# Two GpSimd steps wait for VectorE, and four engines get other orders, in a one-core attention kernel

## The chip, the core and the metric

The kernel runs on one core of a Trainium2 chip. The core has a TensorE (matrix products, PE in the profile, with PEld for its weight loads), a VectorE (DVE), a ScalarE (ACT), a GpSimd (POOL) and a SyncE (SP), which only issues transfers here. Each engine takes its own list of instructions strictly in order and waits for the others by semaphores. The metric is the time of one execution in device microseconds, as the median of several runs. A profiled execution has a span, from its first to its last instruction, and a time of its own, which is a little longer.

## The reference

```python
Q, K, V: (8 batches, 12 heads, 512 rows, 64 columns), float32;  tau = 0.1
Q_norm = Q / (norm(Q, axis=-1) + 1e-10);  K_norm = K / (norm(K, axis=-1) + 1e-10)
scores = Q_norm @ K_norm^T / tau
weights = softmax(scores, axis=-1)
out = weights @ V
```

That is 96 heads of attention with cosine scores. The scores are bounded by 1/tau, so the kernel takes no maximum out of the exponential.

## The kernel before

The 96 heads are worked as 48 pairs, s = 0 to 47. The text names a step by its kind, the pair, and what follows:

- LD.s.w loads Q (w = 0) or K (w = 1) of a pair, LV.s loads V (SyncE, L320 and L323). VC.s copies V to bfloat16 (GpSimd, L582).
- SQ.s squares Q and K (GpSimd, L346, 1024 columns). SSQ.s.w adds up those squares on TensorE for most K halves (8 matmuls, L363); RED.s.w ends the sum on VectorE (L370 after an SSQ, L374 straight from the squares).
- NEW.g.k are the steps of an inverse square root for a group of up to four pairs (VectorE, L399 to L408). Groups from the twelfth on have four pairs: 28 to 31 are group 14, 32 to 35 are 15, 36 to 39 are 16.
- SCL.s.w scales Q or K by the inverse norm to bfloat16 (L432): Q on VectorE, K on GpSimd, except in the pairs that K_ON_DVE lists.
- TR.s.w transposes them on TensorE (four matmuls, L438), EVA.s copies the transposed pair out of PSUM (VectorE, L446).
- SCO.s.c makes the scores of one quarter c of the keys for both heads (two matmuls, L561), EXP.s.c takes their exponential (ScalarE, L577, 1024 columns). There are two score buffers: the scores of one quarter need the exponential of the quarter two earlier to be done.
- PV.s.h.t multiplies by V for one head h and one quarter t of the queries (four matmuls, L594); a 65th column of ones gives the sum of the weights. RCP.s.h inverts the sum (L613), NRM.s.h multiplies by it (VectorE, L615). ST.s stores the pair (SyncE). Each head parity has one PSUM bank for its products, so PV.s.h.0 waits for the NRM of the products that stood there before, and for a RED whose SSQ used a corner of the bank.

In two places ScalarE's work is moved elsewhere. The last quarter of the keys of pairs 30 and 43 has no EXP: SCX makes its scores, X.s.h.k prepares them on VectorE (L496, L499), and a polynomial takes the place of the exponential. For pair 30 (form "B") Y.30.0 to Y.30.2 run on GpSimd (L517, L518), Y.30.3 and Y.30.4 on VectorE (L519). Both of these take two float32 operands of 128 x 1024 from SBUF. Pair 43 (form "A") has Y.43.0 to Y.43.3 on GpSimd, Y.43.4 (L519) and Y.43.5 (L518) on VectorE. PV_LATER puts the products of pair 30 behind those of pair 31.

Nothing is scheduled at run time. A table ORDER gives each engine's list as numbers of the steps in the sequence in which `P.add` made them, and `Program.run` (L52) writes the lists with the waits that each step's `needs` ask for. The order in which TensorE takes its work is such that two to four PV, TR or SSQ steps stand between one SCO and the next; a step among them that has to wait holds up the SCO behind it. The tail is the last pair: its last quarter is exponentiated in three pieces (512, 128 and 384 columns, L572), each with its own products (L630), RCP (L641), NRM (L649, one on ScalarE at L645) and store (L653).

"The head" is what each list holds up to about the seventh pair.

Of the kernel before, what the change touches and what calls it, by code (L numbers as in the profile page):

```python
# [5 lines left out]
ALU = mybir.AluOpType  # L6
# [102 lines left out]
def bass_cosine_similarity_attention_kernel(  # L109
# [10 lines left out]
    NT = SEQ // 128  # L120
# [57 lines left out]
    def key(name, s, *rest):  # L178
        return (name, s) + rest if s >= 0 else None
# [30 lines left out]
    for (s, c), (turns, _) in OFF.items():  # L210
        for h in range(2):
            turn_user.setdefault(turns[h], []).append((s, h))
# [93 lines left out]
    def pair(s):  # L306
# [119 lines left out]
        for w in range(2):  # L426
# [4 lines left out]
                  [("NEW", g, (7 if direct_r(g) else 6) if acts and dve else 6 + w + (dve and w))] + ([("UNIT", s)] if s in off_of and w == 0 else []) + ([("TR", 0, w, 0), ("TR", 0, w, 1)] if s == R_QN else [key("TR", s - R_QN, w)]),  # L431
# [4 lines left out]
            def tr(e, w=w):  # L436
                for t in range(NT):
# [4 lines left out]
            P.add(("TR", s, w), "pe", "tr", T0 - PERIOD + 0.9 * TR_AT[w],  # L442
                  [("SCL", s, w), ("EVA", s - 1) if s > 1 else ("EVA", 0, 0, 1), "eye"]
                  + [x_last(*u) for u in turn_user.get(s - 1, [])[-1:]], tr)
        P.add(("EVA", s), "dve", "eva", T0 - 1.5, [("TR", s, 0), ("TR", s, 1)] + scos(s - R_QT),
              lambda e: e.tensor_copy(  # L446
                  out=qt[iqt][:, :, :, :].rearrange("p w t x -> p (w t x)"),
                  in_=t_ps[:, :, :, :].rearrange("p w t x -> p (w t x)")))
# [30 lines left out]
    def poly(s, c, at):  # L479
# [6 lines left out]
        for h in range(2):  # L486
            users = turn_user[turns[h]]
# [10 lines left out]
            P.add(("X", s, h, 1), "dve", "x1", at + h, [("X", s, h, 0)],
                  lambda e, h=h, z1=z1: e.scalar_tensor_tensor(out=z1, in0=xp[:, h, :], scalar=a0 - LIFT * UNIT, in1=x_ps, op0=ALU.add, op1=ALU.subtract))  # L499
            if form != "D":  # L500
                continue
            two, half = xp[:, h, :].bitcast(bf16), xw[:, h, :]
            chain = [
                lambda e: e.tensor_tensor(out=x_ps, in0=x_ps, in1=x_ps, op=ALU.mult),
                lambda e, two=two, half=half: e.scalar_tensor_tensor(out=half, in0=x_ps, scalar=a3, in1=two, op0=ALU.add, op1=ALU.mult),
                lambda e: e.scalar_tensor_tensor(out=x_ps, in0=x_ps, scalar=2.0 * a1, in1=x_ps, op0=ALU.add, op1=ALU.mult),
                lambda e, h=h, half=half: e.scalar_tensor_tensor(
                    out=et[s % R_ET][:, c, h, :], in0=x_ps, scalar=a1 * a1 + a2, in1=half, op0=ALU.add, op1=ALU.mult)]
            for k, step in enumerate(chain):
                P.add(("X", s, h, k + 2), "dve", "x1", at + h + 0.6 * k,  # L510
                      [("X", s, h, k + 1)] + (done(1) if k == 1 else []) + ([key("PV", s - R_ET, i, NT - 1) for i in range(2)] if k == 3 else []), step)
        if form == "D":
            return
# [107 lines left out]
    def last(s, T0):  # L621
        iq, iet, io = s % R_QK, s % R_ET, s % R_O
        spare = t_ps[:, :, :, :].rearrange("p w t x -> p (w t x)").bitcast(f32)
        for k, (h, lo, hi) in enumerate(PIECES):
            bank = spare if k == 2 else o_ps[h]
            for c in range(NT):
                def pv(e, h=h, lo=lo, hi=hi, c=c, bank=bank):
                    for t in range(lo, hi):
# [8 lines left out]
                           + (([("EVA", s)] if k == 2 else bank_free[s, h]) if c == 0 else [("PV", s, k, c - 1)]), pv)  # L637
# [40 lines left out]
PV_LATER = {30:1}  # L678
EARLY = 4
# [19 lines left out]

def late(s):  # L700
    return LATE * max(0.0, 1 - s / LATE_TO)


def slack(s, most):
# [14 lines left out]
    ),  # L719
    "pool": (  # L720
# [113 lines left out]
```

## Time and profile before

| what | value |
|---|---|
| median of 3 runs | 189.42 us (189.26, 189.42, 190.38) |
| the profiled execution's own time | 190.04 us |
| its span | 188.1 us |
| granted TensorE clock, mean over the span | 0.999 |
| HBM read, written | 37.75 MB, 12.58 MB |
| DVE chain, ACT chain (shares of the chain that ended last) | 63%, 26% |

The page gives each engine's busy time with its share of the span. A group of instructions has its source line, engine, operation, written and read tile, shape, count, then busy time and mean duration, then the idle time of its engine just before it. The timeline gives start and length in us; neighbours of one kind are merged into one row with their count, and a bracket tells the idle time before a row and what ended it. The table of stages gives start and end, length, and the busy time of each engine with its count of instructions. Instructions of one engine overlap at their ends, so a duration is longer than the distance to the next start.

### The profile page before, as it was taken

To read this page: it belongs to the slowest core of one execution; us is meant where nothing else is said; L and a number is where in the kernel's file an instruction comes from. 1 tells how busy PE (TensorE), PEld (TensorE's weight loads), DVE (VectorE), ACT (ScalarE), POOL (GpSimd) and SP (SyncE) were. 2 spreads that over 40 slices of the span, in tenths; PEclk is the share of its full clock that TensorE was granted. 3 is DMA by queue.
4 is the path that set the end of the run, shared out by engine and by line. 5 is a ranking of instruction groups with operands and counts; after the bars stand their busy time and mean duration, and the time that the engine had idled before them with its cause. 6 is when DMAs were issued, how large, how long until landed. Compare 5 with 4: busy or idle time off the path is not lost.

```text
span 188.1 us, 6663 instructions
## 1 busy us (share of the span) xinstructions
PE 176.0 (94%) x2705; PEld 108.9 (58%) x2705; DVE 175.4 (93%) x567; ACT 181.5 (96%) x213; POOL 163.4 (87%) x148
## 2 busy tenths in 40 slices
PE   6898899999998999999999999899999999999993
PEld 2454566666555666656666655466565566556562
DVE  2689999999999999999999999999999999999853
ACT  5799999999999999999999999999999999999993
POOL 5399999999999999999999999999999999298000
PEclk9999999999999999999999999999999999999999
DMA  5999999999999999998999999579971031133334
GB/s 149 345 349 349 349 348 372 377 353 352 353 375 380 379 351 327 345 334 268 315 352 347 360 375 369 183 223 300 357 247 56 6 110 59 57 114 112 116 123 159
DMA packets 52446, 50.76 MB, mean 270 GB/s; under 512 B 3264, under 2 KB 52416, under 8 KB 52416
## 3 DMA queue, kind: packets, MB, share of 16 engines
q1 hardware_dynamic: 51984, 50.05, 81.0%
q8 instruction: 21, 0.34, 0.8%
q10 hardware_dynamic: 432, 0.30, 0.5%
q14 instruction: 9, 0.07, 0.1%
HBM read 37.75 MB, written 12.58 MB: 268 GB/s over the span
## 4 chain that ended last, share of the span: by engine, by line
DVE 63%; ACT 26%; PE 3%; DMA 3%; issue 3%; SPq 1%
ACT et L577 25%; DVE qn L432 14%; DVE ob L615 11%; DVE qt L446 11%; DVE nps L374 10%; DVE rd L613 3%; DMA qk<-in_K_dram 3%; DVE nps L370 3%; DVE nps L399 2%; DVE nps L400 2%; PE ops L594 2%; DVE nps L404 1%; PE scps L561 1%; DVE ys L404 1%; DVE ys L408 1%
## 5 line engine op out<-in xcount | busy, mean ns | idle before, releaser
L577 ACT ACTIVATE et<-scps 128x1024 bf16<-128x1024 f32 x185 | 170.4, 1190 | 0.2
L346 POOL TENSOR_TENSOR sq<-qk 128x1024 bf16<-128x1024 f32 x44 | 85.0, 1943 | 0.1
L561 PE MATMUL scps<-qt 64*128 64x512 bf16 x372 | 72.5, 386 | 4.3 <-ACT et L577 2.5
L594 PE MATMUL ops<-vb,et 128*128 128x65 bf16 x1504 | 73.4, 195 | 1.0 <-DVE ob L615 0.5
L594 PEld LDWEIGHTS ops<-vb,et 128*128 128x128 bf16 x1504 | 55.2, 98 | 31.9 <-issue 18.4
L432 DVE TENSOR_TENSOR qn<-qk,nps 128x512 bf16<-128x512 f32 x61 | 39.9, 676 | 0.6 <-ACT nps L391 0.6
L615 DVE TENSOR_TENSOR ob<-ops,rd 128x256 f32<-128x256 f32 x94 | 38.6, 416 | 0.4
L432 POOL TENSOR_TENSOR qn<-qk,rk 128x512 bf16<-128x512 f32 x33 | 34.2, 1045 | 4.3 <-DVE rk L404 4.1
L438 PE MATMUL tps<-ident,qn 128*128 128x128 bf16 x376 | 33.3, 220 | 0.9 <-DVE qn L432 0.6
L446 DVE COPY qt<-tps 128x1024 bf16<-128x1024 bf16 x47 | 32.0, 681 | 0.2 <-PE tps L438 0.2
L374 DVE TENSOR_REDUCE nps<-sq 128x8 f32<-128x512 bf16 x46 | 30.6, 679 | 0.0
L561 PEld LDWEIGHTS scps<-qt 64*128 64x128 bf16 x372 | 18.2, 92 | 20.6 <-ACT et L577 6.5
L582 POOL TENSOR_SCALAR vb<-vf 128x512 bf16<-128x512 f32 x48 | 29.4, 632 | 0.1
L438 PEld LDWEIGHTS tps<-ident,qn 128*128 128x128 bf16 x376 | 21.6, 98 | 11.7 <-issue 4.9
L363 PE MATMUL ops<-sq,ident 128*128 128x64 bf16 x384 | 19.2, 193 | 1.1 <-POOL sq L340 0.6
L613 DVE RECIPROCAL rd<-ops 128x4 f32<-128x4 f32 x94 | 15.8, 173 | 2.6 <-PE ops L594 2.6
L363 PEld LDWEIGHTS ops<-sq,ident 128*128 128x128 bf16 x384 | 14.2, 98 | 5.5 <-issue 2.0
L370 DVE TENSOR_REDUCE nps<-ops 128x8 f32<-128x64 f32 x46 | 9.8, 216 | 0.0
L400 DVE SCALAR_TENSOR_TENSOR nps<-nps,ys 128x32 f32<-128x32 f32 (+2 forms) x34 | 7.0, 206 | 0.4
L340 POOL TENSOR_TENSOR sq<-qk 128x512 bf16<-128x512 f32 (+1 forms) x5 | 4.7, 954 | 3.0 <-DMA qk<-in_K_dram 2.7
L399 DVE TENSOR_TENSOR nps<-nps,ys 128x32 f32<-128x32 f32 (+2 forms) x34 | 7.0, 206 | 0.3
L192 PE MATMUL ops<-warm_in,ident 128*128 128x512 bf16 x8 | 3.6, 628 | 1.4 <-POOL eps L185 1.4
(67 smaller groups left out, 71.2 us busy)
## 6 DMA issues: line engine op xcount, KB each, us to landing
vf<-in_V_dram SPq DMA_DIRECT2D x48, 256.0 KB, 6.8
qk<-in_Q_dram SPq DMA_DIRECT2D x47, 256.0 KB, 5.5
qk<-in_K_dram SPq DMA_DIRECT2D x47, 256.0 KB, 6.6
out_dram<-ob SPq DMA_DIRECT2D x47, 256.0 KB, 4.2
qk<-in_Q_dram SPq DMA_DIRECT2D x2, 128.0 KB, 2.5
qk<-in_K_dram ACTq DMA_DIRECT2D x2, 128.0 KB, 2.8
out_dram<-ob SPq DMA_DIRECT2D x1, 128.0 KB, 1.7
out_dram<-ob SPq DMA_DIRECT2D x1, 96.0 KB, 1.6
```

Source lines behind the costliest of these rows:

```text
L346: lambda e: e.tensor_tensor(out=sqf, in0=data, in1=data, op=ALU.mult))
L363: last = e.matmul(out=o_ps[bank][:, 320:384], lhsT=ident[:, :], rhs=sq[iqs][:, 8 * w : 8 * w + 8, 8 * k : 8 * k + 8], start=(k == 0), stop ...
L374: lambda e, w=w, dst=dst: e.tensor_reduce(out=dst, in_=sq[iqs][:, 8 * w : 8 * w + 8, :], axis=AX.X, op=ALU.add))
L432: lambda e, w=w, r=r: e.tensor_tensor(out=qn[iqn][:, w].rearrange("p t h d -> p h t d"), in0=qk[iq][:, w].rearrange("p h (t d) -> p h t d" ...
L438: last = e.transpose(t_ps[:, w, t, :], qn[iqn][:, w, t].rearrange("p h d -> p (h d)"), ident[:, :])
L446: lambda e: e.tensor_copy(out=qt[iqt][:, :, :, :].rearrange("p w t x -> p (w t x)"), in_=t_ps[:, :, :, :].rearrange("p w t x -> p (w t x)")))
L561: last = e.matmul(out=sc_ps[:, 2 * b + h, :], lhsT=qt[iqt][64 * h : 64 * h + 64, 1, c, :], rhs=qt[iqt][64 * h : 64 * h + 64, 0, :, :], sta ...
L577: lambda e, c=c, b=b: e.activation(out=et[iet][:, c, :, :], in_=sc_ps[:, 2 * b : 2 * b + 2, :], func=ACT.Exp, scale=math.log(2.0) / UNIT i ...
L582: lambda e: e.tensor_scalar(out=vb[:, iq, :, :, 0:DIM].rearrange("p c h d -> p h c d"), in0=vf[iv][:, :, :].rearrange("p h (c d) -> p h c ...
L594: last = e.matmul(out=o_ps[h][:, 65 * t : 65 * t + 65], lhsT=et[iet][:, c, h, 128 * t : 128 * t + 128], rhs=vb[:, iq, c, h, :], start=(c = ...
L613: (lambda e, h=h, grid=grid: e.reciprocal(out=rd[io][:, h, :], in_=grid[:, :, DIM])))
L615: lambda e, h=k, grid=grid: e.tensor_tensor(out=ob[io][:, h], in0=grid[:, :, 0:DIM], in1=rd[io][:, h, :].unsqueeze(2).to_broadcast([128, N ...
```

## The change

Most lines of the diff change nothing in the built program: a removed polynomial form "D" that no pair used, a way of transposing by DMA for pairs in TURNED, which is empty, loads issued by ScalarE for pairs in BY_SCALAR, which is empty, and the helper `by_pe`, which returns its argument while TURNED is empty. What is left are two added waits and other orders. The set of instructions, their shapes and their engines are the same.

```diff
+    for waits, held in HOLD.items():
+        P.ops[waits].needs.append(held)
     P.run()
...
+HOLD = {("SQ",36,0):("Y",30,3),("VC",44):("Y",30,4)}
...
+TURNED = range(0)
+BY_SCALAR = ()
...
 ORDER = {
     "sp": (
...
-        "428 429 353 471 470 396 430 69 472 504 153 505 547 548 108 581 582 506 624 625 549 658 659 583 700 701 "
+        "428 429 353 471 470 396 430 69 472 504 505 547 548 581 582 506 624 625 549 658 659 583 700 701 626 734 "
...
     "act": (
...
-        "1725 1727 1755 1757 1759 1761 1789 1791 1793 1795 1822 1824 1826 1830 1828 1829 1851 1852 "
+        "1725 1727 1755 1757 1759 1761 1789 1791 1793 1795 1822 1824 1826 1828 1830 1829 1851 1852 "
```

So SQ.36.0 on GpSimd now waits for Y.30.3 on VectorE, and VC.44 on GpSimd for Y.30.4. The other differences are positions in the lists. Counted by place, 116 of SyncE's 193 places hold another step, 89 of GpSimd's 144, 326 of VectorE's 567 and 460 of TensorE's 734; the first of them stand at SyncE's 39th place (LD.12.1 for ST.2), GpSimd's 28th (SCL.7.1 for VC.7), VectorE's 86th (RED.8.0 for SCL.7.0) and TensorE's 91st (TR.7.1 for TR.7.0). ScalarE's list changes in two places at its end: the 512-column piece of the last quarter now comes before the 128-column piece.

The places that matter below, in names:

```
GpSimd around pair 30
before  SCL.29.1 VC.37 VC.36 SCL.31.1 VC.38 SQ.33 SQ.34 SQ.35 Y.30.0 Y.30.1 VC.39 Y.30.2
        SCL.32.1 SQ.36 SCL.34.1 SQ.37 VC.40 SQ.38 SQ.39 SCL.35.1
after   SQ.32 SQ.35 SCL.28.1 VC.35 SCL.29.1 VC.37 VC.34 SCL.31.1 SQ.33 SQ.34 SQ.37 Y.30.0 VC.36 Y.30.1
        Y.30.2 SCL.32.1 SQ.36 SCL.34.1 SCL.35.1 VC.44 VC.43 SQ.39 SQ.38 VC.42 VC.40 VC.45 VC.41
VectorE ahead of NRM.9.0
before  RED.14.0 SCL.12.0 RED.14.1 RCP.8.1 NRM.9.0
after   SCL.12.0 NEW.8.8 RED.14.1 RCP.9.0 SCL.12.1 NRM.9.0 SCL.13.0 EVA.12 RED.14.0
VectorE around Y.30
before  SCL.32.0 NEW.15.8 Y.30.3 RCP.27.1 SCL.33.1 NRM.27.1 EVA.32 SCL.33.0 RCP.28.1 NRM.28.1 RCP.29.0
        SCL.34.0 NRM.29.0 RED.36.1 EVA.33 RCP.29.1 Y.30.4 RCP.31.0 RED.37.1 NRM.29.1 NRM.31.0 EVA.34
after   NEW.15.8 SCL.32.0 Y.30.3 EVA.32 SCL.33.1 RCP.27.1 SCL.33.0 NRM.27.1 SCL.34.0 EVA.33 RCP.29.0 RED.36.1
        NRM.29.0 RCP.28.1 Y.30.4 NRM.28.1 EVA.34 RED.37.0 RCP.31.0 RED.37.1 NRM.31.0 RCP.29.1
TensorE ahead of some scores
before  PV.23.1.2 TR.28.1 TR.28.0 SCO.26.3          after   TR.28.0 TR.28.1 SCO.26.3
before  PV.30.0.0 PV.31.1.0 PV.31.1.1 PV.30.0.1 SCO.33.2 ... PV.31.1.3 SSQ.38.1 PV.32.0.0 SCO.34.0
after   PV.29.1.2 PV.29.1.3 TR.35.1 SCO.33.2 PV.30.0.0 PV.30.0.1 PV.30.0.2 PV.30.0.3 SCO.33.3
        ... PV.32.0.2 PV.32.0.3 SSQ.38.1 SSQ.39.1 SCO.34.2
SyncE ahead of LV.44
before  ST.24 LV.42 ST.21 ST.26 LD.45.0 ST.23 LD.45.1 ST.25 LV.43 LD.46.0 ST.22 LD.46.1 LD.47.0 LV.44
after   LV.42 LD.45.0 LD.45.1 LV.43 LD.46.0 ST.22 ST.23 LD.46.1 ST.21 LD.47.0 LV.44 ST.25 ST.27 ST.26
VectorE's end
before  NRM.46.1 RCP.47.2 RCP.47.0 NRM.47.0 RCP.47.1 NRM.47.1
after   NRM.46.1 RCP.47.0 RCP.47.2 NRM.47.0 RCP.47.1 NRM.47.1
```

More of the change, by code (lines that the diff above doesn't have):

```diff
@@ L211, in bass_cosine_similarity_attention_kernel @@
         for h in range(2):
-            turn_user.setdefault(turns[h], []).append((s, h))
+            turn_user.setdefault(by_pe(turns[h]), []).append((s, h))
+    for users in turn_user.values():
+        users.sort()
     session, attached, early = {}, {}, []
@@ L318, in pair @@
                 continue
-            P.add(("LD", s, w), "sp", "ld1" if s == 1 else "ld", s, [*([("CST", 0, i) if w else ("SCL", 0, 0, i) for i in range(2)] + [("SQ", 0, w, 0), ("SQ", 0, w, 1)] if s == R_QK else [key("SCL", s - R_QK, w), *(squares(s - R_QK, w) if s >= R_QK else [])])],
+            P.add(("LD", s, w), "act" if (s, w) in BY_SCALAR else "sp", "ld1" if s == 1 else "ld", s, [*([("CST", 0, i) if w else ("SCL", 0, 0, i) for i in range(2)] + [("SQ", 0, w, 0), ("SQ", 0, w, 1)] if s == R_QK else [key("SCL", s - R_QK, w), *(squares(s - R_QK, w) if s >= R_QK else [])])],
                   lambda e, w=w, x=x: e.dma_start(out=qk[iq][:, w], in_=src(x, s)),
@@ L430, in pair @@
             P.add(("SCL", s, w), "dve" if dve else "pool", "sclq" if dve else "sclk", T0 - (2.85 if w and not dve else 2.55) - slack(s, M_SCL),
-                  [("NEW", g, (7 if direct_r(g) else 6) if acts and dve else 6 + w + (dve and w))] + ([("UNIT", s)] if s in off_of and w == 0 else []) + ([("TR", 0, w, 0), ("TR", 0, w, 1)] if s == R_QN else [key("TR", s - R_QN, w)]),
+                  [("NEW", g, (7 if direct_r(g) else 6) if acts and dve else 6 + w + (dve and w))] + ([("UNIT", s)] if s in off_of and w == 0 else []) + ([("TR", 0, w, 0), ("TR", 0, w, 1)] if s == R_QN else [key("TR", s - R_QN, w)] if s - R_QN not in TURNED else [("EVA", s - R_QN)]),
                   lambda e, w=w, r=r: e.tensor_tensor(
@@ L440, in tr @@
                 return last
[L442 to L448, printed above, removed]
+            if s not in TURNED:
+                P.add(("TR", s, w), "pe", "tr", T0 - PERIOD + 0.9 * TR_AT[w],
+                      [("SCL", s, w), ("EVA", by_pe(s - 1)) if s > 1 else ("EVA", 0, 0, 1), "eye"]
+                      + [x_last(*u) for u in turn_user.get(by_pe(s - 1), [])[-1:]], tr)
+        if s in TURNED:
+            P.add(("EVA", s), "sp", "trd", s + TURN_AT, [("SCL", s, 0), ("SCL", s, 1)] + scos(s - R_QT),
+                  lambda e: e.dma_start_transpose(
+                      out=qt[iqt][:, :, :, :].rearrange("p w t x -> p (w t) x"),
+                      in_=qn[iqn][:, :, :, :, :].rearrange("p w t h d -> p (w t h d)")), slot=f"qt{iqt}")
+        else:
+            P.add(("EVA", s), "dve", "eva", T0 - 1.5, [("TR", s, 0), ("TR", s, 1)] + scos(s - R_QT),
+                  lambda e: e.tensor_copy(
+                      out=qt[iqt][:, :, :, :].rearrange("p w t x -> p (w t x)"),
+                      in_=t_ps[:, :, :, :].rearrange("p w t x -> p (w t x)")))
         rest(s)
@@ L486, in poly @@
         for h in range(2):
-            users = turn_user[turns[h]]
+            users = turn_user[by_pe(turns[h])]
             before = [x_last(*users[users.index((s, h)) - 1])] if users.index((s, h)) else []
@@ L492, in sco @@
                                 rhs=qt[s % R_QT][64 * h : 64 * h + 64, 0, :, :], start=True, stop=True)
-            P.add(("SCX", s, h), "pe", "sco1", at + h, [("EVA", s), ("EVA", turns[h])] + before, sco)
+            P.add(("SCX", s, h), "pe", "sco1", at + h, [("EVA", s), ("EVA", by_pe(turns[h]))] + before, sco)
             P.add(("X", s, h, 0), "dve", "x1", at + h, [("SCX", s, h)] + done(2),
                   lambda e, h=h: e.tensor_scalar(out=xp[:, h, :], in0=x_ps, scalar1=BIG, scalar2=LIFT * UNIT - BIG, op0=ALU.add, op1=ALU.add))
-            z1 = x_ps if form == "D" else xz[:, h, :]
             P.add(("X", s, h, 1), "dve", "x1", at + h, [("X", s, h, 0)],
[L499 to L513, printed above, removed]
+                  lambda e, h=h: e.scalar_tensor_tensor(out=xz[:, h, :], in0=xp[:, h, :], scalar=a0 - LIFT * UNIT, in1=x_ps, op0=ALU.add, op1=ALU.subtract))
         flat = lambda t: t[:, :, :].rearrange("p h q -> p (h q)")
@@ L636, in last @@
                            ([("EXP", s, c, k)] if c == NT - 1 else exps(s, c)) + [("VC", s)]
-                           + (([("EVA", s)] if k == 2 else bank_free[s, h]) if c == 0 else [("PV", s, k, c - 1)]), pv)
+                           + (([("EVA", by_pe(s))] + [x_last(*u) for u in turn_user.get(by_pe(s), [])[-1:]] if k == 2 else bank_free[s, h]) if c == 0 else [("PV", s, k, c - 1)]), pv)
                 op.count = hi - lo
@@ L678 @@
 PV_LATER = {30:1}
+TURNED = range(0)
+TURN_AT = 6.5
 EARLY = 4
@@ L697, in on_pe, with by_pe @@
     return 0 < s < PE_BOTH or s >= EARLY and (s not in BY_VECTOR if w else s in Q_ON_PE)
+def by_pe(s):
+    while s in TURNED:
+        s -= 1
+    return s
 def late(s):
```

10 lines of the change are left out of this document (4 added, 6 removed), and 122 rows, old and new, of the table ORDER.

## The prediction

> **What bounds the kernel now.** I read the busy table of the page first, then the groups of instructions, then ScalarE's own timeline.
>
> ```profile
> span 188.1 us, 6663 instructions
> PE 176.0 (94%) x2705; PEld 108.9 (58%) x2705; DVE 175.4 (93%) x567; ACT 181.5 (96%) x213; POOL 163.4 (87%) x148
> L577 ACT ACTIVATE et<-scps 128x1024 bf16<-128x1024 f32 x185 | 170.4, 1190 | 0.2
> ```
>
> ScalarE has 185 exponentials (EXP) of one size, and sat idle only 0.2 us before them. A row that shows no idle time can still hide losses, so I look at the ends. The timeline merges neighbours: start, length, count.
>
> ```profile
> 13.17 1.06 ACT L577 ACTIVATE et<-scps 128x1024 bf16<-128x1024 f32 x1
> 13.17 7.69 ACT L577 ACTIVATE et<-scps 128x1024 bf16<-128x1024 f32 x8
> 53.01 1.02 ACT L577 ACTIVATE et<-scps 128x1024 bf16<-128x1024 f32 x1
> 58.65 45.02 ACT L577 ACTIVATE et<-scps 128x1024 bf16<-128x1024 f32 x49
> 132.07 1.02 ACT L577 ACTIVATE et<-scps 128x1024 bf16<-128x1024 f32 x1
> 134.05 1.02 ACT L577 ACTIVATE et<-scps 128x1024 bf16<-128x1024 f32 x1
> 182.38 1.32 ACT L577 ACTIVATE et<-scps 128x1024 bf16<-128x1024 f32 x1
> L577 ACT ACTIVATE et<-scps x185: 1017/1205/1343, 13.2 to 182.4; 128x1024 bf16<-128x1024 f32 x185
> ```
>
> The long row begins with a 1.02 one, so 48 ends are (45.02 - 1.02)/48 = 0.917 us apart. That is the steady pitch. Durations creep from 1.02 to 1.34, and one that falls back to 1.02 came late: up to 0.32 us of a late score is absorbed, the rest is lost. From the first end, 14.23, to the last, 183.70, are 184 steps: 169.47 against 184 x 0.917 = 168.67. So ScalarE lost only 0.80 us:
> - the first eight took 20.86 - 14.23 - 7 x 0.917 = 0.21 too long;
> - from there to the end of the one at 58.65 (42 steps), 59.67 - 20.86 - 38.50 = 0.31, at 53.01 and 58.65;
> - over the last 87 steps, 183.70 - 103.67 - 79.75 = 0.28, at 132.07 and 134.05.
>
> No order behind the head can take out more than 0.80 here. But little is spare elsewhere either:
>
> ```profile
> 90.00:112.00 22.00, 21.29 (x338) 13.35 (x339) 21.86 (x70) 22.00 (x25) 21.98 (x22) 1.00 1.09 353
> 112.00:135.00 23.00, 21.54 (x351) 13.33 (x350) 22.83 (x63) 22.97 (x26) 22.77 (x16) 1.00 0.88 285
> 135.00:160.00 25.00, 24.35 (x381) 15.17 (x377) 25.00 (x79) 25.00 (x29) 24.71 (x21) 1.00 0.32 110
> ```
>
> These stages give the length, then PE, weight loads, DVE, ACT, POOL, the clock, the DMA share and GB/s. VectorE, ScalarE and GpSimd are all full, so a misplaced step on any reaches the end.
>
> **The change, part by part.** No computation is added or removed, and ScalarE's list changes in its last pieces alone.
>
> *The early loss stays.*
>
> ```profile
> 18.07 0.41 PE L363 MATMUL ops<-sq,ident 128*128 128x64 bf16 x8 [0.43 <-POOL sq L346]
> ```
>
> TensorE stood 0.43 before SSQ.5.1, with SCO.2.2 queued behind; both orders agree there. Gain 0.
>
> *The loss at 53.01.* TensorE waited on VectorE's NRM.9.0 (L615):
>
> ```profile
> 51.78 0.39 DVE L615 TENSOR_TENSOR ob<-ops,rd 128x256 f32<-128x256 f32 x1
> 52.22 0.30 PEld L594 LDWEIGHTS ops<-vb,et 128*128 128x128 bf16 x8 [0.31 <-DVE ob L615]
> L374 DVE TENSOR_REDUCE nps<-sq 128x8 f32<-128x512 bf16 x46 | 30.6, 679 | 0.0
> ```
>
> Compared as sets, what leaves the queue ahead of NRM.9.0 is RED.14.0 (0.68) and RCP.8.1, and nothing enters: about 0.7 earlier, against a wait of 0.31. Gone. At 58.65 SCO.13.1 stood behind TR.14.0; ahead of its SCL.14.0 another reduction leaves and a NRM with its RCP enters, so it comes about 0.25 earlier. I book the whole 0.31; if NRMs moved forward push other steps back, it is 0.
>
> *The loss at 132.07 and 134.05*, and the two held steps:
>
> ```profile
> 122.65 1.22 DVE L519 SCALAR_TENSOR_TENSOR xz<-xz,xp 128x1024 f32<-128x1024 f32 x1
> 128.38 0.18 DVE L613 RECIPROCAL rd<-ops 128x4 f32<-128x4 f32 x1
> 128.47 1.66 DVE L519 SCALAR_TENSOR_TENSOR et<-xw,xz 128x1024 bf16<-128x1024 f32 x1
> 129.80 0.62 PE L438 MATMUL tps<-ident,qn 128*128 128x128 bf16 x8
> 131.05 0.66 PE L594 MATMUL ops<-vb,et 128*128 128x65 bf16 x16 [0.30 <-DVE ob L615]
> 173.59 1.22 DVE L519 SCALAR_TENSOR_TENSOR et<-xz,xw 128x1024 bf16<-128x1024 f32 x1
> 121.69 1.04 POOL L432 TENSOR_TENSOR qn<-qk,rk 128x512 bf16<-128x512 f32 x1
> 122.69 2.93 POOL L346 TENSOR_TENSOR sq<-qk 128x1024 bf16<-128x1024 f32 x1
> 126.58 1.89 POOL L346 TENSOR_TENSOR sq<-qk 128x1024 bf16<-128x1024 f32 x1
> 128.44 0.62 POOL L582 TENSOR_SCALAR vb<-vf 128x512 bf16<-128x512 f32 x1
> 129.03 4.71 POOL L346 TENSOR_TENSOR sq<-qk 128x1024 bf16<-128x1024 f32 x2
> ```
>
> SQ.36.0 began at 122.69, 0.04 after Y.30.3, and took 2.93 where another takes 1.89. VC.40 began at 128.44, 0.03 ahead of Y.30.4, which took 1.66 where Y.43.4, with GpSimd idle, takes 1.22. The square behind it took 4.71 - 1.89 = 2.82. Whoever began second lost 0.44 on VectorE, 1.04 and 0.93 on GpSimd. The holds take those pairs apart: VectorE gains 0.44, GpSimd gains 1.97 and waits instead. Before Y.30.0 two copies leave GpSimd's queue and SQ.37.0 enters, 1.89 - 2 x 0.6 = 0.7 later, so SCL.32.1 ends at 123.43 and SQ.36.0 waits 0.44 for Y.30.3's 123.87. SQ.36.0 and two scales (1.89 + 2 x 1.04) then reach 127.84; Y.30.4, ahead of which a NRM and a RCP leave (0.4), would run from 128.05 to 129.27, so VC.44 waits 1.43. Sum 1.87, bounds 0 (VectorE early) and 3.0 (1 us late): GpSimd comes out even. VC.44 moves far forward and needs its load early:
>
> ```profile
> 118.18 4.27 SPq L619 DMA_DIRECT2D out_dram<-ob  x2
> 128.35 0.55 SPq L323 DMA_DIRECT2D vf<-in_V_dram  x1
> vf<-in_V_dram SPq DMA_DIRECT2D x48, 256.0 KB, 6.8
> ```
>
> In before, LV.44 was issued at 128.35, and landed too late for a copy at 129. ST.25 and ST.26 leave the queue ahead of it; the row at 118.18 is a queue that stood about 3.9 (4.27 less an issue) for ST.26, whose NRM.26.1 came late. With that wait behind it, and two issues of about 0.5, LV.44 goes out near 123.5 and lands before 130.3 by the median of 6.8. VC.44 is asked for at 129.3, so between 0 and 1.0 of waiting is left; the stage from 112 moved 285 GB/s where the one before moved 353, so the DMA has room, and I take 0.
>
> TensorE's wait at 131.05 was for NRM.31.0. Ahead of it NRM.29.1 and RCP.29.1 leave, EVA.34 and RED.37.0 enter (+0.76), and 0.44 is saved: 0.3 later, but PV.30.0.0 now stands a score slot (0.92) later. Gone: 0.28, of which I book half, for the next paragraph's reason and because SSQ.38.1 and SSQ.39.1 now share one slot ahead of SCO.34.2.
>
> *A rule against this.* Rows first: SCL.32.1 (121.69, 1.04) ended 0.08 into Y.30.3, without harm. Y.30.2, which comes 0.7 later with the rest of GpSimd's queue, now frees SCL.32.1 and Y.30.3 at about the same time, and no hold covers that pair. The Trainium skill, "SBUF — State Buffer", section "Who interferes with whom", says that a VectorE instruction with two SBUF inputs and a GpSimd one that reads SBUF take one port by turns, whichever issues first holding it for its whole length. By that rule, which the rows above bear out, the hold moves the block and does not end it; the sum would then be the first rival's, and by the harmless row of SCL.32.1 alone it is the forecast's.
>
> *What is late next.* GpSimd. SQ.35.0 enters ahead of SCL.28.1, two copies leave: 0.7 later.
>
> ```profile
> 105.75 2.04 POOL L432 TENSOR_TENSOR qn<-qk,rk 128x512 bf16<-128x512 f32 x2
> 106.47 0.39 PE L561 MATMUL scps<-qt 64*128 64x512 bf16 x2
> 107.47 0.39 PE L561 MATMUL scps<-qt 64*128 64x512 bf16 x2
> ```
>
> SCL.28.1 would end at 107.5, where both transposes of pair 28 must fit between the scores at 106.47 and 107.47. TR.28.1 (four transposes, under half the 0.62 of the eight at 129.80) then pushes the score to about 107.75: 0.28 late, between 0 and 0.28 lost, as the creep absorbs it or not. I book 0.25 for this and other places together.
>
> *VectorE's queue.* A NRM straight behind its own RCP starts 0.20 after it, where another step starts 0.09 after (128.38 to 128.47; 185.31 to 185.51 below). There are 11 such pairs, not 14, and three fewer of other kinds: about 0.6 us less queue, which lengthens leads. Gain on the path 0; it covers the small overlaps above.
>
> *The tail.*
>
> ```profile
> 183.29 1.46 ACT L572 ACTIVATE et<-scps 128x128 bf16<-128x128 f32 x3
> 184.32 0.74 PE L630 MATMUL ops<-vb,et 128*128 128x65 bf16 x16 [0.19 <-DVE ob L615]
> 184.97 0.42 DVE L649 TENSOR_TENSOR ob<-ops,rd 128x256 f32<-128x256 f32 x1
> 185.31 0.17 DVE L641 RECIPROCAL rd<-ops 128x3 f32<-128x3 f32 x1
> 185.51 0.36 DVE L649 TENSOR_TENSOR ob<-ops,rd 128x192 f32<-128x192 f32 x1
> ```
>
> The 512-column piece now comes first, so RCP.47.0 and NRM.47.0 start earlier, and the last RCP, at 185.31, can follow TensorE's end, 185.06. Between 0 (NRM.47.0 now has RCP.47.2 ahead) and 0.25; I take 0.15.
>
> **Sum.** -0.31 - 0.14 + 0.25 - 0.15 = -0.35 us. The profiled execution took 190.04, 1.94 over its span, and lies 0.62 above the median of 189.42; its span would become 187.75, its time 189.7, and the median 189.1.
>
> **Rivals.**
> - *The block moves* (the port mechanism): Y.30.3 starts up to 1.04 after Y.30.2, and EVA.32, SCL.33.1 and SCL.33.0 queue behind it. The 0.14 and VectorE's 0.44 are lost, with 0.2 to 0.3 more at SCO.32.0: 189.5. For it speaks GpSimd's 0.7; against it, that VectorE may arrive first.
> - *GpSimd falls behind* and the kernel is slower. Place: VC.44, VC.43, SQ.39.0, SQ.38.0 behind the second hold. Counted from a Y.30.4 ending at 129.3 they end at 129.3 + 2 x 0.6 + 2 x 1.89 = 134.3, and SSQ.38.1 is wanted at about 135 (EXP.34.2 is due at 134.05 + 2 x 0.917 = 135.9, its score 0.4 ahead of it, two SSQ ahead of that). It decides when Y.30.4 ends, or V 44 lands, later than 130.0. Each us beyond delays SCO.34.2 and, through RED, NEW.16 and EVA.36, SCO.36.0: 1 us costs 0.7 (0.3 absorbed) there, and 0.3 for SCL.28.1 and the lost 0.14 come on top: 190.3; 2 us, 191.3.
> - *The search only moves the waits:* every lost 0.1 comes back at another step: 189.4.
>
> **How the numbers follow.** Forecast 189.1, chance 0.45; block moves, 0.2; GpSimd behind, 0.25; no difference, 0.1. Low end: all 0.59 and the tail's 0.25 won, 188.6, less 0.15 for the scatter of runs (189.26 to 189.42): 188.4. High end: GpSimd behind by 1 us with a little over, 190.5. A measurement tells about 1%, 1.9 us, from no change: faster would need under 187.5, more than ScalarE's whole loss and the tail (chance 0.02); slower, over 191.3, only the 2 us end of the second rival (0.08); within, 0.90.
>
> **What would show it.** Right: no 1.02 exponential near 53, 58 and 132; SQ.36.0 and SQ.38.0 at 1.89; Y.30.4 at 1.22; GpSimd idle about 1.9 us between 122 and 130; the last RCP nearer 185.1. Wrong: Y.30.3 at over 1.22 or waiting on L432; TensorE waiting on GpSimd at pairs 28 or 38; new 1.02 rows.

## The result and the profile after

The changed kernel took 188.70 us (median of 20 runs, 188.38 to 189.56), before 189.24 us in the 20 runs beside it: a ratio of 0.997, 95% interval 0.9956 to 0.9983, or 0.54 us (0.32 to 0.83). That is a small gain: no change lies outside the interval, and the gain is below the 1% that the chances were set by. Forecast were 189.1 against 189.42, a gain of 0.32.

The busy table and the group of exponentials, from the page of the changed kernel:

```profile
span 186.6 us, 6661 instructions
PE 174.7 (94%) x2705; PEld 108.6 (58%) x2705; DVE 174.9 (94%) x567; ACT 181.1 (97%) x213; POOL 161.3 (86%) x148
L568 ACT ACTIVATE et<-scps 128x1024 bf16<-128x1024 f32 x185 | 170.0, 1201 | 0.2 <-PE scps L552 0.2
```

GpSimd lost 2.1 us of busy time and VectorE 0.5, with the same instructions. Nearly all of it is in the two places around pair 30 where instructions of both engines had lasted longer beside each other (1.04 + 0.97 on GpSimd, 0.47 on VectorE; rows below). The profiled execution took 188.64 us, near its median, while before's profiled one took 190.04, 0.80 over the median of its 20 runs. So the two spans (188.1 and 186.6) must not be subtracted. ScalarE's timeline shows why; the last number of a row counts the merged exponentials:

```profile
12.18 5.62 ACT L568 ACTIVATE et<-scps 128x1024 bf16<-128x1024 f32 x6
18.04 164.34 ACT L568 ACTIVATE et<-scps 128x1024 bf16<-128x1024 f32 x179 [0.24 <-PE scps L552]
```

The first exponential began at 12.18 instead of 13.17, although the orders are the same up to there: 0.99 us of the difference of the spans belongs to the head. What the change can move is the stretch from there to the last end, 18.04 + 164.34 - 12.18 = 170.20 us. For before it is 183.70 - 13.17 = 170.53. At the steady pitch it would be the first exponential and 184 steps, 1.06 + 168.67 = 169.73. So before lost 0.80 and the changed kernel 0.47, of which 0.40 are early: the 14th exponential ended at 18.04 + 7.51 = 25.55, against 12.18 + 1.05 + 13 x 0.917 = 25.15.

```profile
18.04 7.51 ACT L568 ACTIVATE et<-scps 128x1024 bf16<-128x1024 f32 x8 [0.24 <-PE scps L552]
```

From there on only 0.07 is lost, near 62 us: EXP.14.2 is a new late one, because PV.13.0.0 ahead of its score waited for VectorE's NRM.12.0. No exponential near 53, 58, 132 or 134 starts late any more.

Around pair 30, GpSimd first, then VectorE:

```profile
119.04 1.89 POOL L509 TENSOR_TENSOR xw<-xw 128x1024 f32<-128x1024 f32 x1
120.89 1.04 POOL L434 TENSOR_TENSOR qn<-qk,rk 128x512 bf16<-128x512 f32 x1
123.25 1.89 POOL L348 TENSOR_TENSOR sq<-qk 128x1024 bf16<-128x1024 f32 x1 [1.31 <-DVE xz L510]
128.43 1.21 POOL L573 TENSOR_SCALAR vb<-vf 128x512 bf16<-128x512 f32 x2 [1.28 <-PE ops L585]
129.60 3.74 POOL L348 TENSOR_TENSOR sq<-qk 128x1024 bf16<-128x1024 f32 x2
```

```profile
121.28 0.69 DVE L434 TENSOR_TENSOR qn<-qk,nps 128x512 bf16<-128x512 f32 x1
121.88 1.22 DVE L510 SCALAR_TENSOR_TENSOR xz<-xz,xp 128x1024 f32<-128x1024 f32 x1
127.05 1.19 DVE L510 SCALAR_TENSOR_TENSOR et<-xw,xz 128x1024 bf16<-128x1024 f32 x1
```

SQ.36.0 takes 1.89 instead of 2.93, the two squares SQ.39.0 and SQ.38.0 3.74 instead of 4.71, Y.30.4 1.19 instead of 1.66. In exchange GpSimd waits 1.31 and 1.28 us. The second wait is put down to TensorE (L585), but the last product that V 44's buffer had to wait for ended at 123.6; what came last was Y.30.4, which ended at 128.24.

The tail:

```profile
181.96 1.47 ACT L563 ACTIVATE et<-scps 128x512 bf16<-128x512 f32 x3
183.26 0.18 DVE L632 RECIPROCAL rd<-ops 128x4 f32<-128x4 f32 x1 [0.32 <-PE ops L621]
183.82 0.17 DVE L632 RECIPROCAL rd<-ops 128x3 f32<-128x3 f32 x1
```

From the last full exponential's end (182.38) to the last RCP are 1.44 us; in before 185.31 - 183.70 = 1.61.

### The profile page after: what moved, and what is told of

Same layout as the page of the kernel before. It is cut to its first block, busy times and chain, and to the rows that moved or that the text cites. A ratio compares the mean times of both kernels' runs of the same rounds, so it can differ in the third digit from the quotient of the medians.

```text
span 186.6 us, 6661 instructions
## 1 busy us (share of the span) xinstructions
PE 174.7 (94%) x2705; PEld 108.6 (58%) x2705; DVE 174.9 (94%) x567; ACT 181.1 (97%) x213; POOL 161.3 (86%) x148
## 4 chain that ended last, share of the span: by engine, by line
ACT 88%; SPq 4%; DMA 4%; POOL 1%; DVE 1%; PE 1%; issue 0%
ACT et L568 88%; DMA qk<-in_K_dram 4%; SPq L322 2%; SPq L325 1%; POOL sq L348 1%; SPq L319 0%; DVE ob L640 0%; ACT et L563 0%; PE ops L365 0%; DVE rd L632 0%; PE scps L552 0%; PE ops L621 0%
## 5 line engine op out<-in xcount | busy, mean ns | idle before, releaser
L348 POOL TENSOR_TENSOR sq<-qk 128x1024 bf16<-128x1024 f32 x44 | 82.6, 1892 | 1.4 <-DVE xz L510 1.3
L585 PE MATMUL ops<-vb,et 128*128 128x65 bf16 x1504 | 72.8, 194 | 0.9 <-DVE ob L606 0.4
L585 PEld LDWEIGHTS ops<-vb,et 128*128 128x128 bf16 x1504 | 55.2, 98 | 30.1 <-issue 17.8
L434 DVE TENSOR_TENSOR qn<-qk,nps 128x512 bf16<-128x512 f32 x61 | 40.4, 676 | 0.6 <-ACT nps L393 0.6
```

What stands on the lines that cost most here:

```text
L348: lambda e: e.tensor_tensor(out=sqf, in0=data, in1=data, op=ALU.mult))
L434: lambda e, w=w, r=r: e.tensor_tensor(out=qn[iqn][:, w].rearrange("p t h d -> p h t d"), in0=qk[iq][:, w].rearrange("p h (t d) -> p h t d" ...
L585: last = e.matmul(out=o_ps[h][:, 65 * t : 65 * t + 65], lhsT=et[iet][:, c, h, 128 * t : 128 * t + 128], rhs=vb[:, iq, c, h, :], start=(c = ...
```

## The experiments

Each kernel ran beside before on one chip; the ratio is to the runs of before beside it, with its 95% interval. Those runs of before had medians of 189.24 to 189.47 us from chip to chip, so a gain in us is given by the ratio, unless two medians are named. The last column is read from the one profiled execution: the stretch from the first full exponential's start to the last one's end, less the 169.73 that it would take at the steady pitch. Two theories stood at the start. A: the other orders carry the gain and the holds only turn blocked time into waiting time. B: the holds carry it.

| kernel | us | ratio to before | stretch of the exponentials, over 169.73 |
|---|---|---|---|
| before | 189.24 | 1 | 0.80 |
| the changed kernel | 188.70 | 0.997 (0.9956 to 0.9983) | 0.47 |
| the same again | 188.68 | 0.9962 (0.9945 to 0.9979) | 0.20 |
| orders alone | 188.82 | 0.9969 (0.9950 to 0.9988) | 0.24 |
| holds alone | 188.96 | 0.9987 (0.9970 to 1.0003) | 1.41 |
| tail alone | 189.16 | 0.9990 (0.9977 to 1.0003) | 0.79 |
| NRM.9.0 first | 189.44 | 1.0005 (0.9983 to 1.0028) | 0.88 |
| first part | 191.81 | 1.0144 (1.0106 to 1.0182) | 2.21 |
| first part, VectorE and TensorE only | 192.92 | 1.0177 (1.0152 to 1.0202) | 4.72 |
| first part, mended | 189.16 | 0.9987 (0.9970 to 1.0004) | 0.47 |
| back part | 189.08 | 0.9986 (0.9972 to 1.0000) | 0.74 |
| scores first | 189.12 | 0.9981 (0.9968 to 0.9994) | 0.39 |
| block | 189.01 | 0.9982 (0.9967 to 0.9998) | 0.56 |
| late hold | 190.43 | 1.0056 (1.0031 to 1.0081) | 2.79 |

**Orders alone.**

```diff
-HOLD = {("SQ",36,0):("Y",30,3),("VC",44):("Y",30,4)}
+HOLD = {}
```

> The changed kernel's orders on all engines, without the two holds. Theory A (the orders carry the gain, the holds are worth nothing): where a hold made GpSimd wait, VectorE's product now makes it wait by itself. SQ.36.0 begins at about 121.9, just behind the start of Y.30.3, takes 2.93 instead of 1.89 and ends near 124.9 (with the hold 125.14); VC.44 begins near 127.1 beside Y.30.4, and one of the two takes longer: VC.44 about 1.8 where it began second, or Y.30.4 1.66 where it began second. Time 188.7 +- 0.15, 0.54 under before. Theory B (the holds carry the gain): Y.30.3 and Y.30.4 take 1.66 or more, exponentials of 1.02 us come back near 134, and the time is that of before, 189.2.

GpSimd's timeline without the holds, then VectorE's Y.30.4:

```profile
121.71 2.96 POOL L348 TENSOR_TENSOR sq<-qk 128x1024 bf16<-128x1024 f32 x1
127.67 1.46 POOL L573 TENSOR_SCALAR vb<-vf 128x512 bf16<-128x512 f32 x2 [1.00 <-DMA vf<-in_V_dram]
129.10 3.74 POOL L348 TENSOR_TENSOR sq<-qk 128x1024 bf16<-128x1024 f32 x2
```

```profile
126.87 1.20 DVE L510 SCALAR_TENSOR_TENSOR et<-xw,xz 128x1024 bf16<-128x1024 f32 x1
```

The kernel took 188.82 us, the changed kernel's time within the intervals: theory A. SQ.36.0 was long again, but it began second (Y.30.3 at 121.70, SQ.36.0 at 121.71), and Y.30.3 kept its 1.22; the square ended at 124.67, earlier than with the hold (125.14). The copy of V 44 came 0.80 into Y.30.4 because its load landed only then. The first hold is worth nothing in this order, and the second hides behind a load.

**Holds alone.** Before's orders on all engines.

```diff
+HOLD = {("SQ",36,0):("Y",30,3),("VC",40):("Y",30,4)}
```

> Before's orders on all engines, with two holds: SQ.36.0 waits for Y.30.3, and VC.40 (the copy that stands just ahead of Y.30.4's time in before's order) waits for Y.30.4. Theory A (holds are worth nothing by themselves): SQ.36.0 and SQ.38.0 take 1.89 instead of 2.93 and 2.82, Y.30.4 1.22 instead of 1.66, and GpSimd waits 1.2 and 1.3 us instead, so that SQ.39.0 ends within 0.4 us of where it did; the time is 189.2 +- 0.15, at most 0.28 better (the loss at 132 and 134 gone by VectorE's 0.44). Theory B: 188.8 or less, near the changed kernel's 188.7.

```profile
124.12 1.89 POOL L348 TENSOR_TENSOR sq<-qk 128x1024 bf16<-128x1024 f32 x1 [1.28 <-DVE rd L604]
126.97 1.89 POOL L348 TENSOR_TENSOR sq<-qk 128x1024 bf16<-128x1024 f32 x1
130.11 0.63 POOL L573 TENSOR_SCALAR vb<-vf 128x512 bf16<-128x512 f32 x1 [1.24 <-DVE rd L604]
```

```profile
128.57 1.37 DVE L510 SCALAR_TENSOR_TENSOR et<-xw,xz 128x1024 bf16<-128x1024 f32 x1
```

The waits and durations came as A said, but Y.30.4 now met the end of SQ.37.0 (126.97 + 1.89 = 128.86) and took 1.37. The stretch of this execution says little about the change: ScalarE's timeline has a wait at pair 5, and the steps ahead of it are before's.

```profile
27.87 24.99 ACT L568 ACTIVATE et<-scps 128x1024 bf16<-128x1024 f32 x27 [0.35 <-PE scps L552]
53.10 130.50 ACT L568 ACTIVATE et<-scps 128x1024 bf16<-128x1024 f32 x142 [0.24 <-PE scps L552]
```

The last row, from EXP.11.3 on, lost 130.50 - 1.02 - 141 x 0.9167 = 0.23 behind its first; the same 142 in before, 183.70 - 53.01 - 1.02 - 129.25 = 0.42. So the holds by themselves take out about 0.2 at pair 30, and the time agrees: 0.25 us by the ratio, with an interval that reaches to zero. The median of 188.96 lies between the two theories' ranges, so it is these rows that speak for A. In before's order they do what the other order does without them, so their gains don't add.

**Tail alone.** In before, as keys of the steps:

```diff
-act: EXP.47.3.2 EXP.47.3.0 EXP.47.3.1
+act: EXP.47.3.0 EXP.47.3.2 EXP.47.3.1
-dve: RCP.47.2 RCP.47.0 NRM.47.0
+dve: RCP.47.0 RCP.47.2 NRM.47.0
-pe: PV.47.2.3 PV.47.1.0 PV.47.0.3 PV.47.1.1
+pe: PV.47.0.3 PV.47.2.3 PV.47.1.0 PV.47.1.1
```

> Before, with the last entries of three orders as in the changed kernel and nothing else: ScalarE's 512-column piece ahead of the 128-column piece, RCP.47.0 ahead of RCP.47.2, PV.47.0.3 ahead of PV.47.2.3. Theory A (the prediction's 0.15): from the last full exponential's end to the end of the span 4.40 becomes 4.2, time 0.15 to 0.2 under before. Rival: the last output pieces' DMAs end where they did, and the difference of the two tails is the scatter of a store: 0.

The last stores' issue, from SyncE's timeline of this kernel:

```profile
184.58 0.87 SPq L653 DMA_DIRECT2D out_dram<-ob  x2
```

It ends 185.45 - 183.03 = 2.42 us behind the last full exponential (12.51 + 170.52 = 183.03). In before it is 186.24 - 183.70 = 2.54:

```profile
185.42 0.82 SPq L653 DMA_DIRECT2D out_dram<-ob  x2
```

The gain is 0.12 by the rows and 0.19 by the ratio, whose interval does not tell it apart from zero. The other profiles do: from the last full exponential's end to the end of the span they have 4.36 or 4.37 us in the six kernels with before's tail and 4.24 or 4.25 in the eight with the changed one. So the tail's gain is 0.12, and a store's scatter is not its cause.

**NRM.9.0 first.** In before, VectorE's order:

```diff
-RED.14.0 RCP.9.0 SCL.12.0 RED.14.1 RCP.8.1 NRM.9.0 RED.15.0 EVA.12
+RCP.9.0 SCL.12.0 RED.14.1 NRM.9.0 RED.14.0 RCP.8.1 RED.15.0 EVA.12
```

> Before, with RED.14.0 and RCP.8.1 moved from ahead of NRM.9.0 to just behind it on VectorE and nothing else. Theory A (the prediction: the wait at 52.22 for NRM.9.0 was the cause of the loss at 53.01): no exponential of 1.02 us near 53, and 0.2 to 0.3 us under before. Rival: the lost time comes back at the next steps (RED.14.0 and with it NEW.8 or EVA.12 late), the exponential at 58.65 or a later one is 1.02 us, and the time is that of before within 0.1.

The rival held: the kernel took 189.44 us, and the ratio's interval lies around 1. TensorE no longer waits for NRM.9.0, but a little later for EVA.12, whose place in VectorE's queue is as before:

```profile
53.67 0.39 PE L561 MATMUL scps<-qt 64*128 64x512 bf16 x2 [0.39 <-DVE qt L446]
```

The late exponential is now EXP.12.0. Taking one step out of the way on a full engine moved the loss on by one step.

**The first part alone, and VectorE and TensorE of it alone.** Before, with the changed kernel's orders to about 75 us on four engines (GpSimd's to 91), and with those of VectorE and TensorE only. The seam is the place in each list where one order goes over into the other.

```diff
-    "dve": before's 244 first entries
+    "dve": the changed kernel's 244 first entries
```

> Before, with the changed kernel's orders on SyncE, GpSimd, VectorE and TensorE in the first part of the pairs alone (to about 75 us, GpSimd's to 91), before's orders behind it, no holds. Theory A (each part of the profile's gains belongs to its own stretch): the losses at EXP.11.3 and EXP.13.1 (53 and 58 us) are gone, EXP.14.2 loses 0.08 to 0.17 as in the changed kernel, those at 132 and 134 stay; 0.15 to 0.3 under before. Rival (the front's gain is given back, as when RED.14.0 and RCP.8.1 alone were moved): within 0.1 of before, with as much lost at other places.

> As the kernel of the first part alone, but only VectorE and TensorE have the changed kernel's orders there; GpSimd and SyncE keep before's. Theory A (the wait at 52.22 was for VectorE's NRM.9.0, so VectorE's order removes it): the losses at EXP.11.3 and EXP.13.1 are gone, as with all four orders. Rival (the orders of squares and copies on GpSimd set when RED.14 and RED.15 can run, so VectorE's order alone makes it wait for GpSimd): TensorE waits for GpSimd's squares between 45 and 60 us, and the time is that of before or longer.

191.81 us (ratio 1.0144, 1.0106 to 1.0182) and 192.92 us (1.0177, 1.0152 to 1.0202): both are slower. The first came out as neither theory had it, the second as its rival, though at another place. From VectorE's timeline of the first and TensorE's of the second:

```profile
82.66 0.70 DVE L374 TENSOR_REDUCE nps<-sq 128x8 f32<-128x512 bf16 x1 [1.99 <-POOL sq L346]
```

```profile
32.45 0.40 PE L438 MATMUL tps<-ident,qn 128*128 128x128 bf16 x4 [1.65 <-POOL qn L432]
```

In the first it was the seam: GpSimd made SQ.24.0 and SQ.26.0 ahead of the SQ.25.0 that VectorE's next reduction wanted. In the second TensorE waited for a GpSimd scale that stands behind a square in before's order, already at pair 7. Four orders are one plan; two of them from one plan and two from another cost 3.4 us by the ratio.

**The first part, mended,** with GpSimd's seam moved to 77 us:

> The kernel of the first part alone once more, with GpSimd's order going over to before's at 77 us, where VectorE's and TensorE's do, instead of at 91 (in the first splice SQ.24.0 and SQ.26.0 stood ahead of SQ.25.0, which VectorE's order of before wanted first, and EXP.20.0 came 1.8 us late). Theory A (the first part's orders take out the losses at EXP.11.3 and EXP.13.1): no late exponential near 80, those at 132 and 134 stay, and the time is 0.15 to 0.3 under before. Rival (the order in front builds no lead that before's back can use, and the gain is given back at the seam or later): 1.02 rows at new places between 60 and 130, time within 0.1 of before or over it.

189.16 us, 0.25 under before, as theory A said, though the interval reaches to zero. The ends of its exponentials show nothing lost at 53 and 58, 0.13 near 62 and 0.20 at EXP.34.0.

**The back part,** the complement, with holds and tail:

> The complement: before's orders in the first part, the changed kernel's behind it, with its two holds and its tail. Theory A: the losses at 53 and 58 us stay (0.31 together), those at 132 and 134 are gone (0.28) and the tail is 0.15 to 0.2 shorter; 0.35 to 0.5 under before. Together with the kernel of the first part alone it makes up the whole change's 0.54 to 0.73. Rival (the back needs the lead that the front's order builds up): a 1.02 row comes back between 100 and 140 us and the gain is 0.2 or less.

189.08 us, 0.27 under before, less than the 0.35 to 0.5 expected: nothing is lost at 132 and 134, but 0.29 at the seam, at 77 us.

```profile
77.19 105.54 ACT L568 ACTIVATE et<-scps 128x1024 bf16<-128x1024 f32 x115 [0.18 <-PE scps L552]
```

Behind its first these 115 lost 105.54 - 1.02 - 114 x 0.9167 = 0.02. The two parts give 0.25 + 0.27, and the whole gave 0.57 and 0.72 by the ratio: they add up, as far as such intervals tell.

**The changed kernel again, and scores first.** The second puts SCO.2.2 ahead of SSQ.5.1 and SCO.2.3 ahead of TR.3.1, to take out the early loss.

```diff
-SSQ.5.1 SCO.2.2 TR.3.0 TR.3.1 SCO.2.3
+SCO.2.2 SSQ.5.1 TR.3.0 SCO.2.3 TR.3.1
```

> The changed kernel unchanged, as the base for the three kernels beside it and as a second profile. Theory A (the early loss hangs on when the first loads land, not on the orders): exponentials end as in the first profile from pair 4 on, with no 1.02 row near 53, 58, 132 or 134; the early loss at EXP.2.2 and EXP.2.3 differs from 0.42, between 0.1 and 0.6. Rival (the early loss is a fixed part of this order): 0.42 again. Time 188.7.

> The changed kernel with two swaps on TensorE: SCO.2.2 ahead of SSQ.5.1, and SCO.2.3 ahead of TR.3.1. Theory A (TensorE's order makes the early loss): EXP.2.2 begins when EXP.2.1 lets it, the 0.42 near 18 to 20 is gone, and the time is 0.15 to 0.4 under the changed kernel. Rival (GpSimd makes it: SCL.3.1 ends behind SQ.5.0, EVA.3 waits for its transposes, and SCO.3.0 for EVA.3): the late exponential is EXP.3.0 in place of EXP.2.2, and the time is within 0.1 of the changed kernel's.

The same kernel again lost next to nothing early, 0.03 up to the 14th exponential (ScalarE's timeline):

```profile
12.19 169.93 ACT L568 ACTIVATE et<-scps 128x1024 bf16<-128x1024 f32 x185
```

Its 170.20 - 169.93 = 0.27 less is not the order. GpSimd's timeline of the first profile, then of the second:

```profile
10.06 2.04 POOL L342 TENSOR_TENSOR sq<-qk 128x512 bf16<-128x512 f32 x2 [0.44 <-DMA qk<-in_Q_dram]
13.36 3.86 POOL L348 TENSOR_TENSOR sq<-qk 128x1024 bf16<-128x1024 f32 x2
```

```profile
9.49 2.04 POOL L342 TENSOR_TENSOR sq<-qk 128x512 bf16<-128x512 f32 x2 [0.40 <-DMA qk<-in_Q_dram]
12.79 3.87 POOL L348 TENSOR_TENSOR sq<-qk 128x1024 bf16<-128x1024 f32 x2
```

Both began their exponentials at 12.18 and 12.19, but pair 3's load let GpSimd go on 0.57 later in the first, so SQ.5.0 ended at 17.22 instead of 16.66, and SSQ.5.1 with SCO.2.2 behind it came late. The other profiles show that this is the cause. SQ.5.0 ended between 4.47 and 5.04 us after the first exponential's start; up to 4.58 the first eight exponentials lost nothing, and from 4.77 on they lost that time less 4.63, to 0.01: 0.14 at 4.77, 0.21 at 4.84 (before), 0.41 at 5.04. This holds in all 13 profiles with this head, whichever order stands behind it. Swapping the two on TensorE did not help: the kernel took 189.12 us, and TensorE's wait turned up two scores later.

```profile
19.62 0.39 PE L552 MATMUL scps<-qt 64*128 64x512 bf16 x2 [0.79 <-DVE qt L455]
```

That is SCO.3.0 behind EVA.3, as the rival had it, but not for its reason: SCL.3.1 was ready at 17.85, and TR.3.1 began at 18.44 because SCO.2.3 now stood ahead of it and itself waited for an exponential. So the swap moved the wait on TensorE from a score to a transpose; whether it costs the 0.44 between the medians, the intervals don't tell.

**Late hold and block.** The first makes GpSimd later, the second makes VectorE's product meet a running scale.

```diff
-HOLD = {("SQ",36,0):("Y",30,3),("VC",44):("Y",30,4)}
+HOLD = {("SQ",36,0):("Y",30,3),("VC",44):("RED",37,0)}
```

```diff
+        ("SCL",32,1):("NEW",15,8)   added to the two holds
```

> The changed kernel with VC.44 held to RED.37.0, a step of VectorE that ends near 129.8, in place of Y.30.4 (128.24): the copies and squares behind it on GpSimd come 1.4 us later. By the prediction's threshold (free until the hold lets go at 130.0): at most 0.1 over the changed kernel. Rival, from the changed kernel's trace (SQ.38.0 ended at 133.34 and SSQ.38.1 began at 133.51, so nothing is spare): SSQ.38.1 and SCO.34.2 come 1.4 us later, 0.1 of it absorbed, TensorE waits for GpSimd's square there, EXP.34.2 is a 1.02 row behind idle time, and the time is 1.0 to 1.3 over the changed kernel.

> The changed kernel with one hold more: SCL.32.1 waits for NEW.15.8, so that it begins near 121.4 instead of 120.89, and Y.30.3, due at 121.88, comes upon it with 0.55 us still to run. By the port mechanism (whichever began first holds VectorE off for its whole length): Y.30.3 takes 1.75 to 1.8 instead of 1.22, EVA.32 and all of VectorE behind it come 0.5 later, and through Y.30.4's hold SQ.38.0 too; 0.2 to 0.5 over the changed kernel. By the harmless row of before alone (overlap costs nothing): Y.30.3 takes 1.22 and the time is the changed kernel's within 0.1.

Late hold, GpSimd's timeline and TensorE's:

```profile
121.30 1.04 POOL L434 TENSOR_TENSOR qn<-qk,rk 128x512 bf16<-128x512 f32 x1
130.60 1.21 POOL L573 TENSOR_SCALAR vb<-vf 128x512 bf16<-128x512 f32 x2 [3.04 <-DVE rd L604]
131.77 3.74 POOL L348 TENSOR_TENSOR sq<-qk 128x1024 bf16<-128x1024 f32 x2
```

```profile
135.57 0.64 PE L365 MATMUL ops<-sq,ident 128*128 128x64 bf16 x16 [1.32 <-POOL sq L348]
```

GpSimd waited 3.04 - 1.28 = 1.76 longer than in the changed kernel, and the time rose by 190.43 - 188.68 = 1.75 us. That is more than the 1.0 to 1.3 that the rival had; the ratio's interval alone allows 1.3 to 2.3. In the profile EXP.34.2 lost 1.54, so only about 0.2 was absorbed there. (EXP.35.0 to EXP.35.3 lost another 0.98, while the granted clock was 0.75 from 135 to 140 us; this execution took 191.54, so its stretch in the table is longer than the medians bear out.) There was hardly any slack, and what came beyond it was lost one for one, as far as such intervals tell.

Block, GpSimd's timeline and VectorE's:

```profile
121.25 1.04 POOL L434 TENSOR_TENSOR qn<-qk,rk 128x512 bf16<-128x512 f32 x1 [0.49 <-DVE nps L406]
```

```profile
121.72 1.66 DVE L510 SCALAR_TENSOR_TENSOR xz<-xz,xp 128x1024 f32<-128x1024 f32 x1
```

Y.30.3 took 1.66 instead of 1.22, as the port mechanism has it. The time rose by 0.33 (189.01 against 188.68; the intervals overlap), and 0.24 of it shows as losses at EXP.32.0 and EXP.32.1, which the changed kernel has not.

## Why the prediction was right, step by step

The direction and the mechanism came out: 0.54 under before (from 0.32 on by the interval) where 0.32 was forecast. Both losses behind the head were met in place and size. The forecast was added up as -0.31 - 0.14 + 0.25 - 0.15 = -0.35; the two profiles of the changed kernel show -0.14 to -0.24 for the first term, -0.28, 0 and -0.12 for the others, -0.54 to -0.64 in all. So the halved term and the one set against it were too cautious by 0.39, the first and the last too hopeful by 0.1 to 0.2, and the forecast is as near as it is because these errors are partly opposite.

- *The early loss stays:* right that the orders don't touch it, wrong that it is a fixed 0.21. It was 0.40 and 0.03 in two executions of one kernel. It depends on when the loads of the first pairs land against ScalarE's start, in before too.
- *The loss at 53 and 58 (0.31):* gone, as booked, with 0.07 to 0.17 given back near 62 us. That new late exponential is one of the prediction's own signs of being wrong: TensorE waited there for a NRM once more. The cause named, RED.14.0 and RCP.8.1 ahead of NRM.9.0, is not enough: moved alone they shifted the loss to EVA.12. The set of steps ahead of a late one is the right thing to compare, but of all the next late steps too, and with GpSimd's order, as the spliced kernels showed. Which further moves did it stays open.
- *The loss at 132 and 134 (0.28, half booked):* all gone. The two reasons for halving it, two SSQ in one slot and a NRM later by 0.3, cost nothing. TensorE's timeline shows the slot with both:

```profile
133.51 0.63 PE L365 MATMUL ops<-sq,ident 128*128 128x64 bf16 x16
134.08 0.39 PE L552 MATMUL scps<-qt 64*128 64x512 bf16 x2
```

  SCO.34.2 came 0.2 late, and the creep of the durations absorbed it.
- *SCL.28.1 and others (+0.25):* did not come. Counted against the exponentials SCL.28.1 was later by 0.4, where 0.7 were forecast, and both transposes still fitted ahead of the score (TensorE's timeline):

```profile
105.89 0.74 PE L440 MATMUL tps<-ident,qn 128*128 128x128 bf16 x8
106.57 0.39 PE L552 MATMUL scps<-qt 64*128 64x512 bf16 x2
```

  The score ended at 106.96 and its exponential could start at 107.00, 0.94 behind the one ahead of it: under 0.1, which the creep absorbed.
- *The holds:* VectorE's gain (1.66 - 1.19 = 0.47 against 0.44) and GpSimd's durations came as forecast. The waits were 1.31 + 1.28 = 2.59 instead of 1.87, within the bound of 3.0. Counted against the exponentials there, which ended 1.03 earlier than in before, SCL.32.1 came only 0.2 later where 0.7 were booked, and Y.30.3 0.25 later where nothing was; so the first wait was 1.31 instead of 0.44. "GpSimd comes out even" holds to 0.3: against the orders alone, again counted against the exponentials, SQ.36.0 to SQ.38.0 ran that much later, at no cost. LV.44's issue ended at 121.04, before the 123.5 forecast, and V 44 had landed at 126.13.
- *The block* did not come by itself: Y.30.3 stood behind two NEW and a scale of VectorE's, so SCL.32.1 had only 0.05 left to run when it began. Made to come, it cost 0.33, where the rival's price was 189.5 - 189.1 = 0.4. The Trainium skill, "SBUF — State Buffer", section "Who interferes with whom", gives the port to the one that issued first; these traces agree as to who is held up, but the price was always less than the rest of the other instruction (below). The Trainium skill says there "for the whole instruction" of VectorE's two-port modes, and of two inputs in SBUF only that they contend; "its whole length" is the prediction's reading of the two together.
- *GpSimd behind:* the place was right (SSQ.38.1, SCO.34.2), the threshold and price too kind. Forecast were 0.7 of slack behind Y.30.4, and of what came beyond it 0.3 absorbed. In the changed kernel SQ.38.0 ended at 133.34 and SSQ.38.1 began at 133.51, so the slack was under 0.2, and 1.76 us cost 1.75. SQ.38.0 came where it was booked (134.37 on before's time, 134.3 booked); it was SSQ.38.1 that was wanted half a us earlier than the 135 booked, which had been counted from EXP.34.0's start in before, a late one. That the change stayed clear of this was luck: by that price, an estimate, a Y.30.4 later by 0.7 us would have cost the whole gain.
- *VectorE's queue:* the lists have 15 and 12 pairs of a NRM straight behind its own RCP, the last pair's counted, and not 14 and 11; the difference of three stands. No run isolates it.
- *The tail (0.15):* 0.12 to the end of the span, in every profile; to the last RCP the rows give 0.17.

## What to carry to other kernels

A wait put in by hand to keep two engines from colliding is worth nothing where the instruction that is held would have come second anyway: it then waits for about as long as it would have been held up. Run the order without the holds before crediting them. On engines that are all full, moving one step out of a late step's way moved the loss to the next step; here only the orders of all engines together took it out. Subtract the head before comparing two profiled spans: here it was 1.0 of 1.5 us.

## What the runs showed of the hardware

Where a VectorE product with both inputs in SBUF and a GpSimd instruction overlap, the one that began second took longer by the overlap less about 0.14 us, in either direction. (Of Y.30.3's two inputs only xz is float32; xp is read as bfloat16, other than is said ahead of the prediction. Both lie in SBUF.) SQ.36.0 in before: 122.65 + 1.22 - 122.69 = 1.18 of overlap, 2.93 - 1.89 = 1.04 longer. Without the holds: 121.70 + 1.22 - 121.71 = 1.21 and 2.96 - 1.89 = 1.07. Y.30.3 in the block: 121.25 + 1.04 - 121.72 = 0.57 and 1.66 - 1.22 = 0.44. Y.30.4 with the holds alone: 0.29 and 0.15 to 0.18. All 14 profiles agree: overlaps of 0.29 to 1.21 cost themselves less 0.11 to 0.14, and those of 0.05 to 0.13, as SCL.32.1's of 0.08 in before and 0.05 after, cost 0.01 at most. An estimate from these rows is that up to 0.14 us is free.

The first exponential of this kernel began between 12.18 and 13.39 us in executions with the same head, and the landing of the first loads decided another 0 to 0.4 us behind it. This scatter of 1.2 us is larger than all that the orders won.
